# Layer 0 of a two-layer decoder trunk: tokens from a feature-major copy, first projection in a score bank, one insertion of attention work per projection

## The chip, the cores and the metric

The kernel runs on one core of one Trainium2 chip, in one launch. The metric is the device time of that core in microseconds (us). Engines: TensorE (PE; its weight loads, PEld, run beside its matmuls), VectorE (DVE), ScalarE (ACT), GpSimd (POOL), and the queue of SyncE (SP), which here only issues DMAs.

## The reference, cut to what matters

The input x is 256 tokens by 1024 features. Layer 0 is RMSNorm, stick-breaking attention with 16 heads of 64, a residual, then RMSNorm and a squared-ReLU MLP. Shared keys and values, a second layer of sparse attention with its own MLP, and a final norm follow; the change does not touch them.

```
def rms_norm(x, g):
    y = x * rsqrt(mean(x * x, axis=-1) + 1e-5)
    return y * g

def stick_breaking_attention(h, w_qkv, w_o):
    q, k, v = split(h @ w_qkv)                    # 16 heads of 64
    z = (q @ k.T) / 8                             # per head
    log_1m = where(causal, log_sigmoid(-z), 0)    # causal: key < query
    excl = reversed_cumsum(log_1m) - log_1m
    a = where(causal, exp(log_sigmoid(z) + excl), 0)
    return (a @ v) @ w_o

h = x + stick_breaking_attention(rms_norm(x, g0), w_qkv, w_o)
h = h + mlp(rms_norm(h, g1))
...
```

## The kernel before

Every large product is made of three: both factors are split into a high part that TensorE takes in one pass and the rest (h and l), and `mm3` (lines 131 to 134) adds h*h, h*l and l*h. Weights come from memory as f32 tiles `raw`; `split` (line 86) cuts one half of such a tile at a time: ScalarE casts it to `wh` (line 96), VectorE subtracts to `wl` (line 97). Each of the three has three buffers. `fetch` (line 75) issues the load of the next tile on SP; it is called when a tile's second half has been split, so the load waits until VectorE has read the tile three places ahead. `step` splits a half if the split is not yet three tiles ahead of the tile in use, `W(i)` splits up to tile i.

`layer0` (line 314) begins with eight matmuls on zeros (`warm`). Tokens are loaded token-major into `hres` in four pieces (line 337), which is also the residual. `xt_tr` (line 188) turns them on TensorE, 8 transposes per half of the features, and `xt_evac` (line 198) multiplies by the norm's gain out of PSUM and splits the result: ScalarE writes the high part (line 204), VectorE the rest (line 205), into `xa`. Then come two projections:

- Values: `v_proj(i)` (line 323) takes piece i of wv. `V_CUT` lists the pieces as (first slice, slices); a slice is 128 features. Per slice there are 12 matmuls of 512 columns, into four PSUM banks `pv`, one per 128 tokens t and half n of the output. Between, ScalarE squares `hres` with a sum (`sq`, line 176), VectorE makes the variance, GpSimd the power (`r`, line 185), and two small products (`pr`, line 361) spread 1/rms over the partitions, from which VectorE makes `rbq`. The four banks are then scaled into `v0` by ScalarE (line 367).
- Queries and keys: eight projections `proj(p)` (line 374), one per pair of heads, each 8 slices of 6 matmuls of 256 columns into one bank `qk`; VectorE scales it into `qkT` (line 385).

The attention of earlier pairs is put between the slices of a projection. `scores(p)` (line 388): TensorE makes z, VectorE caps it into `sbe` (line 404), ScalarE takes exp and ln(1+.) into `sbs` (lines 408, 409), VectorE scans it and subtracts (lines 410, 411), ScalarE takes the last exp (line 412). `turn(p)` (line 415): six transposes into two banks `pa`, copied to `sbt`, one by ScalarE and one by VectorE (lines 426, 424). `values(p)` (line 429): eight matmuls into `po`, split into `oT` by ScalarE and VectorE (lines 213, 214). `inside(n)` (line 441) says where: in projection n, before slice 2 the scores of pair n-1 and the values of pair n-3, before slice 5 the turn of pair n-2. What is left over stands in the output projection (line 454).

PSUM has 8 banks in two rings of four: `bank` (projections, pv, qk, acc) and `bank2` (z, pa, po, pt, pr and the MLP's pu). The order on an engine is made by a scheduler from the written order, and an engine runs its instructions strictly in that order.

## Time and profile before

| what | value |
|---|---|
| runs | 646.24 us median of 3 (646.06 to 646.59) |
| profiled execution | 646.55 us, of which the span from first to last instruction 644.8 us |
| TensorE (PE) busy | 625.1 us, 97% of the span |
| PE weight loads | 530.0 us, 82% |
| VectorE | 438.9 us, 68% |
| ScalarE | 347.5 us, 54% |
| GpSimd | 58.2 us, 9% |
| mean granted TensorE clock | 0.996 of full speed |
| DMA | 106.81 MB, 166 GB/s over the span |

Busy time is a union of instructions, so an engine that is 97% busy has 3% of gaps, and where they lie is read from stretches of the span, not from this table. A clock of 1.00 is 2.4 GHz and of 0.50 is 1.2 GHz. Starts in a timeline are us from the first instruction; a matmul's listed duration is longer than the distance to the next one's start, since matmuls overlap, so a cost per matmul is read from starts. A line's bracket tells how long the engine had stood idle and what ended that.

### The profile page before, as it was taken

Reading aid. Unit: us, or ns where it says so; the run is one execution under the profiler, and the core shown is the slowest. Engines: PE = TensorE matmul, PEld = TensorE weight load, DVE = VectorE, ACT = ScalarE, POOL = GpSimd, SP = SyncE. Lnnn points to the kernel's source line nnn. Section 1 sums busy time; section 2 is a strip of 40 time slices with the busy share of each in tenths; the row PEclk is TensorE's granted clock in tenths of the full one; section 3 lists DMA queues with packets and bytes.
Section 4 is the critical chain, followed back from the end, with each engine's and each line's share of the span. In section 5 each row is a group of like instructions: output and inputs, shape, how many; then the busy total and the mean of one; then the engine's idle time right before and its main releaser. Section 6 shows DMA issues by size and latency. Waiting matters only on the chain.

```text
span 644.8 us, 9082 instructions
## 1 busy us (share of the span) xinstructions
PE 625.1 (97%) x3552; PEld 530.0 (82%) x3552; DVE 438.9 (68%) x638; ACT 347.5 (54%) x596; POOL 58.2 (9%) x100
## 2 busy tenths in 40 slices
PE   8999899999999999999999999999999999999995
PEld 5889887888888888888889987777888888888884
DVE  4768887676666565656899879763776566656564
ACT  5665565564444544444847767762564444444433
POOL 1000000000000000000133344550000000000000
PEclk8999999999999999999999999999999999999999
DMA  8753223535555555553465752001545455555501
GB/s 304 282 226 132 104 100 125 195 131 201 200 187 199 193 196 195 194 195 134 142 241 177 254 191 82 18 2 66 190 148 206 176 201 188 196 197 195 197 0 66
DMA packets 16891, 106.81 MB, mean 166 GB/s; under 512 B 2256, under 2 KB 2512, under 8 KB 4944
## 3 DMA queue, kind: packets, MB, share of 16 engines
q1 hardware_dynamic: 15696, 104.92, 45.4%
q10 hardware_dynamic: 1152, 1.31, 0.6%
q8 instruction: 28, 0.46, 0.3%
q14 instruction: 15, 0.12, 0.1%
HBM read 105.17 MB, written 1.05 MB: 165 GB/s over the span
## 4 chain that ended last, share of the span: by engine, by line
PE 79%; DVE 10%; ACT 4%; issue 3%; POOL 2%; DMA 2%; POOLq 0%; SPq 0%; ACTq 0%; DVEq 0%
PE pu L137 27%; PE acc L132 11%; PE acc L133 11%; PE acc L134 11%; DVE wl L97 3%; PE po L137 2%; PE pk L134 2%; PE pk L132 2%; PE pk L133 2%; DVE sbs L410 2%; PE pv L132 1%; PE pv L133 1%; PE pv L134 1%; PE z L137 1%; ACT wh L96 1%
## 5 line engine op out<-in xcount | busy, mean ns | idle before, releaser
L97 DVE TENSOR_TENSOR wl<-raw,wh 128x1024 fp32r<-128x1024 f32 (+3 forms) x202 | 234.6, 1197 | 122.7 <-ACT wh L96 122.4
L96 ACT CAST wh<-raw 128x1024 fp32r<-128x1024 f32 (+3 forms) x202 | 198.1, 1024 | 119.5 <-PE acc L134 52.1
L137 PE MATMUL pu<-xn,wh 128*128 128x512 f32 x512 | 130.1, 392 | 0.6 <-DVE xn L205 0.6
L137 PEld LDWEIGHTS pu<-xn,wh 128*128 128x128 f32 x512 | 93.8, 188 | 19.6 <-DVE xn L205 1.8
L132 PE MATMUL acc<-wh,hh 128*128 128x512 f32 x256 | 100.2, 391 | 0.0
L133 PE MATMUL acc<-wl,hh 128*128 128x512 f32 x256 | 100.0, 391 | 0.0
L134 PE MATMUL acc<-wh,hl 128*128 128x512 f32 x256 | 99.5, 390 | 0.0
L137 PEld LDWEIGHTS pu<-xn,wl 128*128 128x128 f32 x512 | 71.0, 190 | 5.0
L137 PE MATMUL pu<-xn,wl 128*128 128x256 f32 x512 | 74.0, 282 | 0.0
L134 PEld LDWEIGHTS acc<-wh,hl 128*128 128x128 f32 x256 | 48.1, 188 | 10.6 <-DVE hl L294 0.4
L132 PEld LDWEIGHTS acc<-wh,hh 128*128 128x128 f32 x256 | 48.2, 188 | 9.6 <-ACT hh L293 0.6
L133 PEld LDWEIGHTS acc<-wl,hh 128*128 128x128 f32 x256 | 48.2, 188 | 8.8
L293 ACT CAST hh<-ms 128x512 fp32r<-128x512 f32 x32 | 19.9, 621 | 64.7 <-DVE ms L289 64.7
L287 ACT COPY mr<-pu 128x256 f32<-128x256 f32 x64 | 23.6, 369 | 28.9 <-PE pu L137 28.9
L132 PE MATMUL qk<-xa,wh 128*128 128x256 f32 x128 | 37.3, 291 | 0.0
L134 PE MATMUL qk<-xa,wl 128*128 128x256 f32 x128 | 36.3, 284 | 0.0
L133 PE MATMUL qk<-xa,wh 128*128 128x256 f32 x128 | 36.2, 283 | 0.0
L294 DVE TENSOR_TENSOR hl<-ms,hh 128x512 fp32r<-128x512 f32 x32 | 22.1, 692 | 19.9 <-ACT hh L293 19.9
L288 DVE TENSOR_TENSOR mu<-pu,mr 128x256 f32<-128x256 f32 x64 | 26.7, 418 | 5.8 <-ACT mr L287 5.8
L780 POOL TENSOR_TENSOR pe<-pe,rs 128x256 f32<-128x256 f32 (+1 forms) x32 | 27.1, 866 | 23.5 <-DVE rs L776 19.9
L132 PE MATMUL acc<-wh,oT 128*128 128x512 f32 x64 | 25.9, 405 | 0.0
L132 PEld LDWEIGHTS qk<-xa,wh 128*128 128x128 f32 x128 | 24.5, 191 | 1.0 <-issue 0.9
(188 smaller groups left out, 922.8 us busy)
## 6 DMA issues: line engine op xcount, KB each, us to landing
raw<-in_w SPq DMA_DIRECT2D x64, 1024.0 KB, 4.8
raw<-in_wqk SPq DMA_DIRECT2D x8, 1024.0 KB, 4.9
raw<-in_wo SPq DMA_DIRECT2D x8, 1024.0 KB, 4.8
raw<-in_wkv SPq DMA_DIRECT2D x6, 1024.0 KB, 4.8
raw<-in_cw SPq DMA_DIRECT2D x4, 1024.0 KB, 4.8
raw<-in_wv SPq DMA_DIRECT2D x3, 1024.0 KB, 6.4
raw<-in_wqb SPq DMA_DIRECT2D x2, 768.0 KB, 4.1
raw<-in_wqc SPq DMA_DIRECT2D x2, 768.0 KB, 6.1
```

Source lines behind the costliest of these rows:

```text
L96: nc.scalar.copy(h[:, r], raws[j][:, r])
L97: nc.vector.tensor_sub(lo[:, r], raws[j][:, r], f32(h[:, r]))
L132: nc.tensor.matmul(o, a[0], b[0], start=first, stop=False, skip_group_check=True)
L133: nc.tensor.matmul(o, a[0], b[1], start=False, stop=False, skip_group_check=True)
L134: nc.tensor.matmul(o, a[1], b[0], start=False, stop=last, skip_group_check=True)
L137: nc.tensor.matmul(o, a, b, start=first, stop=last, skip_group_check=True)
L287: nc.scalar.copy(r[:, q], pu[f][:, 256:512])
L288: nc.vector.tensor_add(u[:, q], pu[f][:, 0:256], r[:, q])
L293: nc.scalar.copy(hh, sv)
L294: nc.vector.tensor_sub(hl, sv, f32(hh))
L410: nc.vector.tensor_tensor_scan(s[:, ::-1], s[:, ::-1], go_on[:, ::-1], 0.0, OP.add, OP.mult)
L780: nc.gpsimd.tensor_tensor(s, s, rs[:, t, :][:, :, None].to_broadcast([P, 2, n]), op=OP.mult)
```

## The change

- The input gets a second layout, `xcols`: features on partitions, 8 slices of 256 tokens, made on the host from x. `x_load` brings slices 0 to 3 one by one (128 KB each) and 4 to 7 together into `xin`; `x_cut` multiplies by the gain and splits, from SBUF. The transposes of layer 0's first norm and their PSUM tiles go. There are 13 warm matmuls instead of 8.
- wv comes in six pieces instead of five (slices 0, 1, 2, 3 alone, then 4-5 and 6-7); from the third piece on two halves are split per slice; a slice runs output half by output half, with both token halves in each.
- `hres`, the constants and the identity are loaded on SP after the third piece's work is written; the identity came on ScalarE's queue before.
- The first projection's bank comes from `bank2`; the values' banks come from `bank`, but for the last two pairs.
- Scores, turn and values are put together, before slice 5 of a projection (slice 2 in projection 1); both copies of a turn are ScalarE's. The output projection takes the leftover of pairs 7, 6 and 5 in one place.

```diff
--- before.py
+++ after.py
@@ -24,7 +24,7 @@
 DFF = 4096
 NFC = 16
 NGN = 6
-V_CUT = ((0, 1), (1, 1), (2, 2), (4, 2), (6, 2))
+V_CUT = ((0, 1), (1, 1), (2, 1), (3, 1), (4, 2), (6, 2))
 EPS = 1e-5
 NEG = -1e30
 GELU_C = 2.0 * 0.7978845608028654
@@ -37,7 +37,7 @@
 
 
 @with_exitstack
-def hybrid_kernel(ctx, tc, x, eye, gcols, gfin, wqk, wv, wo0, wkv, wqa, wqb, wqc, wo1, w1, w2, cw1, cw2, cpos, gate_b, consts, out):
+def hybrid_kernel(ctx, tc, x, xcols, eye, gcols, gfin, wqk, wv, wo0, wkv, wqa, wqb, wqc, wo1, w1, w2, cw1, cw2, cpos, gate_b, consts, out):
     nc = tc.nc
 
     cp = ctx.enter_context(tc.tile_pool(name="cp", bufs=1))
@@ -156,7 +156,6 @@
     zero = cp.tile([P, 512], BF16, name="zero")
     nc.vector.memset(zero, 0.0)
     ident = cp.tile([P, P], F32, name="ident")
-    nc.scalar.dma_start(ident, eye)
     hres = [cp.tile([P, D], F32, name=f"hres{t}") for t in range(T)]
     gc = cp.tile([P, NGN * NK], F32, name="gc")
     nc.scalar.dma_start(gc, gcols)
@@ -314,7 +313,7 @@
     def layer0(ap):
 
         warm = bank2("warm")
-        for i in range(8):
+        for i in range(13):
             mm(warm, zero[:, 0:P], zero, True, True)
         xt = xt_tiles("a")
         v = big([P, T, D], F32, "v0")
@@ -324,27 +323,48 @@
             w = W(i_v[i])
             k0, m = V_CUT[i]
             for kk in range(m):
-                step()
+                step(2 if i >= 2 else 1)
                 k = k0 + kk
-                for t in range(T):
-                    for n in range(2):
+                for n in range(2):
+                    for t in range(T):
                         mm3(pv[t][n], tok(xt, k, t), cut(w, kk * D + n * 512, kk * D + (n + 1) * 512),
                             k == 0, k == NK - 1)
 
-        pts = []
-        for half in range(2):
-            for t in range(T):
-                nc.sync.dma_start(hres[t][:, half * 512:(half + 1) * 512], x[t * P:(t + 1) * P, half * 512:(half + 1) * 512])
-            fetch()
-        pts.append(xt_tr(0))
-        xt_evac(pts[0], 0, 0, xt)
+        xin = big([P, NK, T * P], F32, "xin")
+
+        def x_load(k, m):
+            nc.sync.dma_start(xin[:, k:k + m, :].rearrange("p k q -> p (k q)"), xcols[:, k * T * P:(k + m) * T * P])
+
+        def x_cut(k, m):
+
+            for k in range(k, k + m):
+                g = gc[:, k:k + 1]
+                nc.scalar.activation(xt[0][:, k, :], xin[:, k, :], AF.Copy, scale=g)
+                nc.vector.scalar_tensor_tensor(xt[1][:, k, :], xin[:, k, :], g, f32(xt[0][:, k, :]),
+                                               op0=OP.mult, op1=OP.subtract)
+
+        x_load(0, 1)
+        fetch()
+        x_load(1, 1)
+        fetch()
+        x_load(2, 1)
+        fetch()
+        x_load(3, 1)
+        x_cut(0, 1)
         W(i_v[0])
+        x_cut(1, 1)
+        v_proj(0)
+        x_load(4, 4)
+        x_cut(2, 1)
+        v_proj(1)
+        x_cut(3, 1)
+        v_proj(2)
         nc.sync.dma_start(cst, consts)
-        fetch()
-        pts.append(xt_tr(1))
-        v_proj(0)
-        v_proj(1)
-        xt_evac(pts[1], 1, 0, xt)
+        nc.sync.dma_start(ident, eye)
+        for t in range(T):
+            nc.sync.dma_start(hres[t], x[t * P:(t + 1) * P, :])
+        x_cut(4, 4)
+        v_proj(3)
         nc.gpsimd.tensor_copy(cbf, cst[:, 0:2 * P])
 
         go_on = ap.tile([P, 2 * ROW], BF16, name="go_on", bufs=1)
@@ -352,16 +372,15 @@
         nc.gpsimd.memset(go_on.rearrange("p (h c) -> p h c", h=2)[:, :, 2 * SEG - 1:ROW:SEG], 0.0)
         nc.gpsimd.tensor_copy(ident_r, ident)
         nc.gpsimd.tensor_copy(cmb, cst[:, C_CM:C_CM + 30])
-        v_proj(2)
+        v_proj(4)
         rstd = [rstd_of(hres[t]) for t in range(T)]
-        v_proj(3)
         rbq = ap.tile([P, 2, T * P], F32, name="rbq", bufs=1)
         pr = bank2("pr")
         for t in range(T):
             mm(pr[:, t * P:(t + 1) * P], rstd[t].to_broadcast([P, P]), ident, t == 0, True)
         nc.vector.tensor_scalar(rbq[:, 0, :], pr[:, 0:T * P], 0.125, None, op0=OP.mult)
         nc.vector.tensor_copy(rbq[:, 1, :], pr[:, 0:T * P])
-        v_proj(4)
+        v_proj(5)
         for t in range(T):
             for n in range(2):
                 nc.scalar.activation(v[:, t, n * 512:(n + 1) * 512], pv[t][n], AF.Copy, scale=rstd[t])
@@ -372,7 +391,8 @@
         live = {}
 
         def proj(p, hooks={}):
-            qk = bank("qk")
+
+            qk = bank("qk") if p else bank2("qk")
             w = W(i_qk[p])
             for k in range(NK):
                 if k % 4 == 0:
@@ -420,15 +440,12 @@
                 for i, b in enumerate((2, 0, 1)):
                     c = hd * ROW + b * SEG
                     nc.tensor.transpose(pt[:, i * P:(i + 1) * P], e[:, c:c + P], ident)
-                if hd:
-                    nc.vector.tensor_copy(at[:, hd, :], pt[:, 0:384])
-                else:
-                    nc.scalar.copy(at[:, hd, :], pt[:, 0:384])
+                nc.scalar.copy(at[:, hd, :], pt[:, 0:384])
             live[p] = at
 
         def values(p):
             a = live.pop(p)
-            po = bank2("po")
+            po = bank2("po") if p >= NP - 2 else bank("po")
             for b in range(2):
                 for hd in range(2):
                     r = slice(hd * DH, (hd + 1) * DH)
@@ -439,19 +456,12 @@
 
 
         def inside(n):
-            h = {}
-            if n >= 1:
-                h.setdefault(2, []).append(lambda: scores(n - 1))
-            if n >= 3:
-                h.setdefault(2, []).append(lambda: values(n - 3))
-            if n >= 2:
-                h.setdefault(5, []).append(lambda: turn(n - 2))
-            return h
+            return {2 if n == 1 else 5: [lambda f=f, p=n - d: f(p) for d, f in ((1, scores), (2, turn), (3, values)) if n >= d]}
 
         for n in range(NP):
             proj(n, inside(n))
         xn = xt_tiles("n")
-        out_proj(oT, i_o0, {(0, 0, 1): [lambda: scores(NP - 1), lambda: values(NP - 3)], (0, 0, 3): [lambda: turn(NP - 2)],
+        out_proj(oT, i_o0, {(0, 0, 2): [lambda: scores(NP - 1), lambda: turn(NP - 2), lambda: values(NP - 3)],
                             (0, 1, 1): [lambda: values(NP - 2)],
                             (1, 0, 0): [lambda: turn(NP - 1)], (1, 0, 1): [lambda: values(NP - 1)],
                             (1, 1, 2): [lambda: xt_evac(xt_tr(0), 0, 1, xn)]})
@@ -948,6 +958,7 @@
     wqs = [np.concatenate([wq[:, :256], wq[:, 1024:]], 1), wq[:, 256:640], wq[:, 640:1024]]
     f = {
         "x": cont(a["x"][0]),
+        "xcols": cont(a["x"][0].T.reshape(NK, P, T * P).transpose(1, 0, 2).reshape(P, NK * T * P)),
         "eye": np.eye(P, dtype=np.float32),
         "gcols": cont(np.concatenate([a["norm_gain"].reshape(4, D), a["kv_norm"][None], a["final_norm"][None]], 0)
                       .reshape(NGN, NK, P).transpose(2, 0, 1).reshape(P, NGN * NK)),
```

How this moves instructions shows at three places. First SP's queue at the start of the program, from the third issue on, before (x2 is two in a row):

```order
L81 DMA raw<-in_wv 128x512
L82 DMA raw<-in_wv 128x512
L337 DMA hres_72<-in_x 128x512
L337 DMA hres_73<-in_x 128x512
L84 DMA raw<-in_wv 128x1024
L84 DMA raw<-in_wv 128x2048
L342 DMA cst<-in_consts 128x744
L84 DMA raw<-in_wv 128x2048 x2
L84 DMA raw<-in_wqk 128x2048 x8
```

and now, from the eighth issue on:

```order
L336 DMA xin<-in_xcols 128x256
L84 DMA raw<-in_wv 128x1024
L336 DMA xin<-in_xcols 128x1024
L84 DMA raw<-in_wv 128x2048 x2
L84 DMA raw<-in_wqk 128x2048
L362 DMA cst<-in_consts 128x744
L363 DMA ident<-in_eye 128x128
L365 DMA hres_71<-in_x 128x1024
L365 DMA hres_72<-in_x 128x1024
L84 DMA raw<-in_wqk 128x2048 x7
```

The loads of the tokens for the residual (hres) stood at the head, two of the four ahead of these rows, and now stand behind all of wv, the first wqk, the constants (cst) and the identity; ahead of the rows stand now the first slice of xin, both halves of wv's first piece, and then slices of xin and pieces of wv in turn.

Second, VectorE in the middle of the projections, from one pair's cap (sbe from z) through its scan (sbs) to the next pair's cap, before:

```order
L404 TENSOR_TENSOR sbe_657<-z0_651,cst_76 128x3x128
L404 TENSOR_TENSOR sbe_657<-z1_652,cst_76 128x3x128
L214 TENSOR_TENSOR oT_320<-po_667,oT_320 128x256
L410 SCALAR_TENSOR_TENSOR sbs_661<-sbs_661,go_on_191 128x774
L424 COPY sbt_696<-pa_702 128x384
L411 TENSOR_TENSOR sbe_657<-sbe_657,sbs_661 128x774
L385 TENSOR_TENSOR qkT_725<-qk_634,rbq_278 128x512
L97 TENSOR_TENSOR wl_822<-raw_595,wh_821 128x1024
L404 TENSOR_TENSOR sbe_750<-z0_744,cst_76 128x3x128
L404 TENSOR_TENSOR sbe_750<-z1_745,cst_76 128x3x128
L97 TENSOR_TENSOR wl_822<-raw_595,wh_821 128x1024
```

and now:

```order
L424 TENSOR_TENSOR sbe_777<-z0_771,cst_75 128x3x128
L424 TENSOR_TENSOR sbe_777<-z1_772,cst_75 128x3x128
L213 TENSOR_TENSOR oT_325<-po_798,oT_325 128x256
L430 SCALAR_TENSOR_TENSOR sbs_781<-sbs_781,go_on_224 128x774
L405 TENSOR_TENSOR qkT_823<-qk_732,rbq_283 128x512
L431 TENSOR_TENSOR sbe_777<-sbe_777,sbs_781 128x774
L97 TENSOR_TENSOR wl_827<-raw_577,wh_826 128x1024 x2
L424 TENSOR_TENSOR sbe_870<-z0_864,cst_75 128x3x128
L424 TENSOR_TENSOR sbe_870<-z1_865,cst_75 128x3x128
```

The copy of the turn (sbt) is gone, qkT of the next pair stands ahead of the subtraction into sbe, and both halves of the weight (wl) stand ahead of the next cap; before, one of them stood behind the cap in this round, and both ahead of it in the next.

Third, ScalarE in the same place, from one pair's ln (the first row) to the next pair's ln (sbs is exp and ln, sbe the last exp), before:

```order
L409 ACTIVATE sbs_754<-sbs_754 128x774
L426 COPY sbt_789<-pa_790 128x384
L412 ACTIVATE sbe_750<-sbe_750 128x774
L96 CAST wh_914<-raw_688 128x1024 x2
L213 CAST oT_320<-po_853 128x256
L408 ACTIVATE sbs_847<-sbe_843 128x774
L409 ACTIVATE sbs_847<-sbs_847 128x774
```

and now:

```order
L429 ACTIVATE sbs_781<-sbs_781 128x774
L96 CAST wh_826<-raw_577 128x1024 x2
L432 ACTIVATE sbe_777<-sbe_777 128x774
L443 COPY sbt_880<-pa_881 128x384
L443 COPY sbt_880<-pa_886 128x384
L428 ACTIVATE sbs_874<-sbe_870 128x774
L212 CAST oT_325<-po_891 128x256
L429 ACTIVATE sbs_874<-sbs_874 128x774
```

The weight's casts (wh) stand between ln and the last exp, two turn copies follow that, and the cast of oT stands between exp and ln. Before, there was one turn copy, behind ln, the casts stood behind the last exp, and the cast of oT ahead of exp.

## Rows read from the trace of the kernel before

**Rows 1.** Windows: busy us (instructions) of PE, PEld, DVE, ACT, POOL; clock, DMA, GB/s.
```profile
60.00:80.00 20.00, 18.10 (x154) 16.73 (x153) 16.48 (x21) 11.17 (x16) 0.32 (x3) 1.00 0.36 124
```

**Rows 2.** Timeline of the start: start us, duration, engine, line, instruction, [idle before].
```profile
0.73 0.86 SPq L337 DMA_DIRECT2D hres<-in_x  x2
...
1.19 3.52 PE L137 MATMUL warm<-zero 128*128 128x512 bf16 x8 [1.19 <-DVE zero L157]
...
5.15 0.98 PE L195 MATMUL pt<-ident,hres 128*128 128x128 f32 x7 [0.33 <-DMA hres<-in_x]
...
6.67 0.62 ACT L96 CAST wh<-raw 128x512 fp32r<-128x512 f32 x1 [4.66 <-DMA raw<-in_wv]
...
7.71 0.64 PE L132 MATMUL pv<-wh,xa 128*128 128x512 f32 x1 [1.58 <-ACT xa L204]
...
12.42 0.39 PE L132 MATMUL pv<-wh,xa 128*128 128x512 f32 x1
...
17.84 1.06 ACT L176 ACTIVATE sq<-hres 128x1024 f32<-128x1024 f32 x1
...
19.69 1.16 POOL L185 TENSOR_TENSOR r<-v,cst 128x1 f32<-128x1 f32 x2 [5.27 <-DVE v L180]
```

**Rows 3.** Windows of one microsecond at the start, columns as in rows 1.
```profile
6.00:7.00 1.00, 0.13 (x2) 0.00 (x0) 0.00 (x0) 0.33 (x1) 0.00 (x0) 1.00 1.01 289
...
8.00:9.00 1.00, 1.00 (x5) 0.75 (x4) 1.00 (x4) 1.00 (x4) 0.00 (x0) 0.50 0.99 336
...
11.00:12.00 1.00, 1.00 (x7) 0.91 (x7) 0.25 (x1) 0.75 (x2) 0.00 (x0) 0.83 0.91 374
```

**Rows 4.** Timeline of PE through the projections, columns as in rows 2.
```profile
32.62 0.28 PE L132 MATMUL qk<-xa,wh 128*128 128x256 f32 x1
...
38.37 0.28 PE L132 MATMUL qk<-xa,wh 128*128 128x256 f32 x1
...
59.62 0.82 PE L422 MATMUL pa<-ident,sbe 128*128 128x128 f32 x6
...
60.19 0.36 PE L132 MATMUL qk<-xa,wh 128*128 128x256 f32 x1
...
64.16 0.92 PE L137 MATMUL z<-qkT 64*128 64x256 f32 x8
...
65.01 0.87 PE L137 MATMUL po<-sbt,v 128*64 128x256 f32 x8
...
65.81 0.39 PE L132 MATMUL qk<-xa,wh 128*128 128x256 f32 x1
...
74.25 0.92 PE L137 MATMUL z<-qkT 64*128 64x256 f32 x8 [1.77 <-DVE qkT L385]
...
98.71 0.40 PE L132 MATMUL acc<-wh,oT 128*128 128x512 f32 x1
```

**Rows 5.** Timeline of DVE through the projections, columns as in rows 2.
```profile
65.35 2.36 DVE L97 TENSOR_TENSOR wl<-raw,wh 128x1024 fp32r<-128x1024 f32 x2 [1.25 <-ACT wh L96]
...
67.62 1.02 DVE L404 TENSOR_TENSOR sbe<-z,cst 128x384 f32<-128x384 f32 x2
...
70.50 1.77 DVE L410 TENSOR_TENSOR_SCAN sbs<-sbs,go_on 128x774 f32<-128x774 f32 x1 [1.53 <-ACT sbs L409]
...
72.19 0.53 DVE L424 COPY sbt<-pa 128x384 f32<-128x384 f32 x1
...
72.64 0.96 DVE L411 TENSOR_TENSOR sbe<-sbe,sbs 128x774 f32<-128x774 f32 x1
...
73.51 0.68 DVE L385 TENSOR_TENSOR qkT<-qk,rbq 128x512 f32<-128x512 f32 x1
...
103.08 1.02 DVE L404 TENSOR_TENSOR sbe<-z,cst 128x384 f32<-128x384 f32 x2
```

**Rows 6.** Timeline of ACT through the projections, columns as in rows 2.
```profile
66.17 0.36 ACT L213 CAST oT<-po 128x256 fp32r<-128x256 f32 x1
...
68.74 0.85 ACT L408 ACTIVATE sbs<-sbe 128x774 f32<-128x774 f32 x1 [2.21 <-DVE sbe L404]
```

## The prediction

> **What bounds the kernel now.** I read the windows first, then the timeline of the start, then the timelines of the three busy engines through layer 0's projections. From 60 to 80 us TensorE is busy 18.10 of 20 us, VectorE 16.48 and ScalarE 11.17 [rows 1]: TensorE has gaps there, and VectorE, which shows 82%, is the one to suspect. The rest of the kernel is matmul back to back, so what the change saves before the first MLP should stay saved; I found no later wait that would swallow some us.
>
> The start: the first matmul that counts, pv, begins at 7.71, after a 1.58 us wait for ScalarE's token cut, and at 12.42 the tenth starts [rows 2]. From there to the first qk at 32.62 [rows 4] 87 pv and the small pr group take 20.20 us, 0.232 us per pv. The nine before took 4.71 us instead of 9 x 0.232 = 2.09: 2.6 us lost, to transposes in between, waits for the first cuts, and the clock.
>
> The projections: from 32.62 to 98.71 [rows 4] eight of them take 66.1 us. TensorE's own work in them: a projection is 48 matmuls in 5.75 (32.62 to 38.37), a z group costs 0.85 (64.16 to 65.01), a po group 0.80 (to 65.81), a pa group 0.57 (59.62 to 60.19) [rows 4]. With 7 z, 5 po and 6 pa: 46.0 + 5.95 + 4.0 + 3.4 = 59.4. So 6.7 us are waits; the longest shown is z waiting 1.77 for qkT [rows 4]. Behind it is VectorE's order. Its round from one cap of scores to the next takes (103.08 - 67.62) / 4 = 8.87 us [rows 5], where a full TensorE period is 5.75 + 0.85 + 0.80 + 0.57 = 7.97. In the round VectorE stands idle 1.25 us for weight casts and 1.53 us for exp and ln [rows 5].
>
> **The change, part by part.**
>
> *Tokens from xcols.* The 16 transposes ahead of pv go, and ScalarE and VectorE cut from SBUF, eight pairs as before. The first half weight is now second on SP's queue, behind 128 KB. Before, it was third, behind 512 KB; it let ScalarE start at 6.67, and pv followed 1.04 later [rows 2]. The nearest row for the new place is the second 256 KB load of before, also issued second (0.73, two issues in 0.86), which let TensorE go on at 5.15 [rows 2]. So the first pv comes at 5.15 + 1.04 = 6.2. Bounds: 7.7 (nothing gained) and 5.5 (if half the bytes ahead matter). Then 96 pv and pr: 96 x 0.232 = 22.3. Of the 2.6 us lost, the transposes go, the clock should stay up (below), and the waits for VectorE's first cuts stay: I take a third, 0.8, between ends of 0 and 2.6. First qk at 6.2 + 22.3 + 0.8 = 29.3, against 32.62: **3.3 us** earlier. By the ends: 5.5 + 22.3 = 27.8 to 7.7 + 22.3 + 2.6 = 32.6.
>
> The Trainium skill has a rule for such a load ("DMA: Bandwidth & Descriptors", the section on the two cost components): about 2 us plus the bytes at 436 GB/s, given for the other descriptor path. An estimate from it lands that half weight 2.6 us after its issue at 1.16, at 3.8, and would make the start 1.4 us better still. The trace disagrees: the load of that size in that place released TensorE only at 5.15, so the sum keeps the row.
>
> *Five more warm matmuls.* The eight take 3.52 us, 0.44 each, about half the rate of the later pv; the granted clock was 1.00 from 6 to 7, but 0.50 (1.2 GHz) from 8 to 9, and 0.83 from 11 to 12 as it came back [rows 3]. Before it fell, TensorE had been busy 0.13 of a microsecond from 6 to 7 [rows 3]. Five more reach to 6.9 at 0.44, or 5.8 at twice the rate, so pv follows almost directly and I expect no fall. They cost nothing: TensorE has no data then.
>
> *Residual tokens, consts and ident late.* hres is now issued behind all of wv and the first wqk. Who needs it: sq, then r on GpSimd, then pr, which stands on TensorE behind all pv. From sq's start at 17.84 to r's end at 20.85 it took 3.0 us [rows 2]. Bytes up to hres: 1.05 MB xcols, 4.19 wv, 1.05 wqk, 0.45 consts and ident, 1.05 hres, together 7.8 MB. At 289 GB/s [rows 3] from 2 us on, that ends at 29; at 374 [rows 3], at 22.9. I take 25 (the fuller rate holds once loads are large), so r is ready at 28, before the last pv at about 29: no cost. Above 26, each us is a us of TensorE idle, and ScalarE, queued behind sq, casts the second wqk later; that has 5.75 us of slack, one projection. The sixth piece of wv costs one more issue, and the sizes of the pieces hide in the same stream.
>
> *One insertion per projection.* z, pa and po now stand together at slice 5. Two things follow. qkT gains three slices, 3 x 0.72 = 2.2 us, so z's waits (1.77 for one) go. In their place pa of a pair comes one full period after its z: 7.97 us later. What must fit between: cap, exp and ln, 2.88 (67.62 to 70.50 [rows 5]), with the oT cast, 0.33 of it exposed (0.36 long [rows 6]), now between them; the scan 1.69, qkT 0.61 (now ahead of the subtract), the subtract 0.87 [rows 5], and the last exp 0.85, as long as the first [rows 6], with 0.1 for the hand-overs: 7.33. That leaves 0.64 of slack.
>
> *The turn's copy to ScalarE, casts ahead of the last exp.* VectorE loses a copy, 0.45 (72.19 to 72.64), and the 1.25 idle for casts [rows 5], since ScalarE casts while VectorE scans. Its round becomes 2.88 + 0.33 + 1.69 + 0.61 + 0.87 + 2.27 (two wl, 65.35 to 67.62 [rows 5]) = 8.65. That is more than 7.97: VectorE still sets the pace, and TensorE waits 0.68 per period, now at pa for the last exp. The slack delays it once: between the second and third z there is no po yet (7.17), VectorE needs 8.32, the lag of 1.15 exceeds 0.64 by 0.5; then four periods at 0.68. Waits 0.5 + 2.7 = 3.2 instead of 6.7: 3.5 us gained. The output projection pays part back, since z and pa of the last pairs meet the lag again: I take one to two waits of 0.68, 1.0. Net **2.5 us**, ends 0 (round as before) and 6.7 (TensorE's own pace).
>
> *Banks.* qk of the first projection in a score bank and po in projection banks: the score banks then turn over 4 a period for 4 buffers. No wait on a bank shows in the rows, so I put it at nothing; what covers it is that caps and copies end long before the next insertion. Without that cover, pa would wait for a cap, 0.5 per period.
>
> Sum: 3.3 + 2.5 = 5.8. The profiled execution took 646.55 with a span of 644.8; less 5.8 it is 640.75, and the median of the runs stands 0.31 below it: **640.4**.
>
> **The rivals.**
> 1. *The clock falls at the start anyway.* Pv starts in bits, and the granted clock fell in before, too, after partial work. In the Trainium skill, "TensorE: Matmul & The Clock Gate" (table "Why this matters for your kernels") ties a drop to a long idle gap; by that rule the forecast stands. Here it fell after a gap of 1.58 us, so the row speaks for this rival. Price: half rate from 8 to 11.4, 1.7 us less half a us that waits there would have cost anyway, 1.2: 641.6.
> 2. *The loop gains nothing.* ScalarE now has two turn copies and the oT cast ahead of ln; if they delay exp by 0.2 per round, the round is 8.87 again and only the start is gained: 642.9. For it: VectorE's round hardly falls. Against: the copies wait on pa, which ends before the caps do.
> 3. *TensorE reaches its own pace in the loop*: another 3.2 gone, 637.2. Against it: 8.65 over 7.97.
> 4. *Slower: the residual tokens come too late.* Place: pr, behind the last pv, and all of ScalarE behind sq. It decides from a landing after 29, where the start's gain is used up (r at 32). At 31: r at 34, first qk at 34.5, 1.9 worse; TensorE idle for 5 us starts again at half clock, 1.7; the value evacuation and the third pair's casts then delay the first z by about 1.1; less the loop's 2.5: +2.2, 648.4. For it: a megabyte more ahead, in an interval where the queues are always full. Against: 289 GB/s held only in the first microseconds.
>
> **How the numbers follow.** A difference of 0.2%, 1.3 us, is about what a measurement of this kernel can tell from none. Chances: forecast 0.54 (639.2 to 641.4), rival 1 0.19, rival 2 0.13, rival 3 0.07, rival 4 0.07. Faster by over 0.2% means below 644.9: forecast, 1 and 3, most of 2, together 0.88; within 0.2% 0.06 (the weak end of 2, the mild end of 4); slower 0.06. For 8 in 10 the range reaches from 638.4, the forecast's better end with a little of rival 3, to 644.4, rival 2 with a start 1.5 worse.
>
> **What would show it.** Right: first pv near 6.2, first qk near 29.3, no wait before pr, granted clock 1.00 from 8 to 11; no z wait for qkT in the middle projections, pa waiting about 0.7 for the last exp in each, caps 8.65 apart, the output projection starting some 62.6 after the first qk. Wrong: a TensorE wait at pr for r of over 1 us, caps 8.9 or 8.0 apart, or waits of pa or po for a bank.

## The result, and the profile after

The changed kernel took 641.07 us (median of four runs: 642.27, 639.96, 640.21, 641.93) against 646.25 (646.06 to 646.59) of the kernel before: a ratio of 0.992, with a 95% interval of 0.9897 to 0.9942. That is 5.2 us less; the forecast was 640.4. The profiled execution is the slowest of the four, 642.27, with a span of 640.4, so it stands 4.28 below that of before, 4.4 by the spans. One of the seven executions of the last experiment, the profiled one, had a mean granted clock of 0.85 and took 688.36 us, and one of the kernel before beside the experiments took 3523.38; both are left out, and nothing is read from the trace of the first.

Three instants cut the path of TensorE:

| us | before | after, profiled | after, a second profiled execution |
|---|---|---|---|
| first qk | 32.62 | 31.20 | 28.95 |
| output projection starts (first acc) | 98.71 | 93.58 | 91.53 |
| MLP starts (first pu) | 126.83 | 122.65 | 120.59 |
| the eight projections, qk to acc | 66.09 | 62.38 | 62.58 |
| the output projection, acc to pu | 28.12 | 29.07 | 29.06 |

The second execution is that of an experiment below, beside which the kernel before had a median of 645.46. So the start gave 1.42 in one execution and 3.67 in the other, the projections 3.7 and 3.5, and the output projection took 0.95 back. From the first pu to the end of the span it is 518.0 before and 517.8 after: what was saved stayed saved.

The windows of after, in the stretch of [rows 1] and in the first microseconds of [rows 3], with two more (busy us of PE, PEld, DVE, ACT, POOL, then clock, DMA share, GB/s):

```profile
60.00:80.00 20.00, 20.00 (x169) 18.44 (x168) 16.55 (x19) 13.07 (x19) 0.22 (x2) 1.00 0.37 138
...
6.00:7.00 1.00, 1.00 (x4) 0.64 (x3) 1.00 (x3) 0.58 (x2) 0.00 (x0) 1.00 0.96 327
8.00:9.00 1.00, 1.00 (x6) 0.81 (x6) 0.11 (x1) 0.76 (x2) 0.00 (x0) 1.00 1.06 397
11.00:12.00 1.00, 1.00 (x6) 0.84 (x5) 1.00 (x3) 0.43 (x1) 0.00 (x0) 1.00 1.06 352
...
15.00:16.00 1.00, 1.00 (x7) 0.80 (x6) 1.00 (x4) 0.67 (x2) 0.00 (x0) 1.00 0.65 147
```

TensorE has no gap left from 60 to 80 (18.10 busy before), the clock stays at 1.00, and in one microsecond the DMAs move 147 GB/s, less than half of what the other rows of the start show. The timeline of after's start and output projection, PE, ACT and POOL (columns as in [rows 2]):

```profile
1.19 5.73 PE L137 MATMUL warm<-zero 128*128 128x512 bf16 x13 [1.19 <-DVE zero L157]
6.36 0.94 PE L132 MATMUL pv<-wh,xa 128*128 128x512 f32 x1
...
19.46 1.19 PE L132 MATMUL pv<-wh,xa 128*128 128x512 f32 x4 [1.50 <-ACT wh L96]
...
30.83 0.61 PE L137 MATMUL pr<-ident,r 128*128 128x128 f32 x4
31.20 0.36 PE L132 MATMUL qk<-xa,wh 128*128 128x256 f32 x1
...
93.58 0.40 PE L132 MATMUL acc<-wh,oT 128*128 128x512 f32 x1
...
98.15 0.88 PE L442 MATMUL pa<-ident,sbe 128*128 128x128 f32 x6 [0.80 <-ACT sbe L432]
...
122.65 0.39 PE L137 MATMUL pu<-xn,wh 128*128 128x512 f32 x1
...
5.16 0.50 ACT L342 ACTIVATE xa<-xin,gc 128x256 fp32r<-128x256 f32 x1
...
18.37 2.00 ACT L96 CAST wh<-raw 128x1024 fp32r<-128x1024 f32 x2 [2.70 <-DMA raw<-in_wv]
...
25.68 1.06 ACT L175 ACTIVATE sq<-hres 128x1024 f32<-128x1024 f32 x1 [0.34 <-DMA hres<-in_x]
...
28.38 0.55 POOL L184 TENSOR_TENSOR r<-v,cst 128x1 f32<-128x1 f32 x1 [0.73 <-DVE v L179]
```

The first pv shows no wait: it stands behind the last of the 13 warm matmuls, although ScalarE's first cut, xa, had ended at 5.66. The values stop for 1.50 us at the fifth piece of wv, whose cast waited for its load; pr follows the last pv directly, since r was ready at 28.93. One round of the loop in after, first PE, then VectorE, then ScalarE:

```profile
63.68 0.92 PE L137 MATMUL z<-qkT 64*128 64x256 f32 x8
64.53 0.88 PE L442 MATMUL pa<-ident,sbe 128*128 128x128 f32 x6
65.34 0.87 PE L137 MATMUL po<-sbt,v 128*64 128x256 f32 x8
66.14 0.39 PE L132 MATMUL qk<-xa,wh 128*128 128x256 f32 x1
...
72.08 0.92 PE L137 MATMUL z<-qkT 64*128 64x256 f32 x8
...
65.73 1.02 DVE L424 TENSOR_TENSOR sbe<-z,cst 128x384 f32<-128x384 f32 x2
67.99 0.42 DVE L213 TENSOR_TENSOR oT<-po,oT 128x256 fp32r<-128x256 f32 x1 [1.24 <-ACT oT L212]
68.74 1.77 DVE L430 TENSOR_TENSOR_SCAN sbs<-sbs,go_on 128x774 f32<-128x774 f32 x1 [0.33 <-ACT sbs L429]
70.43 0.67 DVE L405 TENSOR_TENSOR qkT<-qk,rbq 128x512 f32<-128x512 f32 x1
71.01 0.96 DVE L431 TENSOR_TENSOR sbe<-sbe,sbs 128x774 f32<-128x774 f32 x1
71.88 2.35 DVE L97 TENSOR_TENSOR wl<-raw,wh 128x1024 fp32r<-128x1024 f32 x2
74.15 1.02 DVE L424 TENSOR_TENSOR sbe<-z,cst 128x384 f32<-128x384 f32 x2
...
63.58 0.85 ACT L432 ACTIVATE sbe<-sbe 128x774 f32<-128x774 f32 x1 [1.41 <-DVE sbe L431]
...
66.84 0.85 ACT L428 ACTIVATE sbs<-sbe 128x774 f32<-128x774 f32 x1 [0.87 <-DVE sbe L424]
```

TensorE's round is 72.08 - 63.68 = 8.40 with no idle time in it, VectorE's 74.15 - 65.73 = 8.42, where it was 8.87 by [rows 5]; that is the mean of rounds of 7.6 and 10.1 us in turn. VectorE follows one chain, cap, (exp and ln on ScalarE), scan, qkT, subtract, two wl, cap, and waits only for ScalarE, 1.57 us. The last exp ends at 64.43 and pa starts at 64.53, so the two engines meet there.

TensorE's waits between first qk and first acc (us in total, times, longest), before:

```profile
PE z L137 <- DVE qkT L385: 4.4, 4, 1.8
```

and after:

```profile
PE pa L442 <- ACT sbe L432: 0.3, 1, 0.3
```

So TensorE's own work in the eight projections was 66.1 - 4.4 = 61.7 before and is 62.4 - 0.3 = 62.1 after.

### The profile page after: what moved, and what is told of

Same layout as the page of the kernel before. It is cut to its first block, busy times and chain, and to the rows that moved or that the text cites. A ratio compares the mean times of both kernels' runs of the same rounds, so it can differ in the third digit from the quotient of the medians.

```text
span 640.4 us, 9068 instructions
## 1 busy us (share of the span) xinstructions
PE 624.8 (98%) x3541; PEld 527.9 (82%) x3541; DVE 435.6 (68%) x632; ACT 350.5 (55%) x606; POOL 59.6 (9%) x100
## 3 DMA queue, kind: packets, MB, share of 16 engines
q10 hardware_dynamic: 1008, 1.25, 0.5%
## 4 chain that ended last, share of the span: by engine, by line
PE 75%; DVE 12%; ACT 4%; DMA 4%; issue 3%; POOL 1%; SPq 0%; POOLq 0%; ACTq 0%; DVEq 0%
PE pu L137 27%; PE acc L132 11%; PE acc L133 11%; PE acc L134 11%; DVE wl L97 5%; PE po L137 2%; DMA raw<-in_wv 2%; DVE sbs L430 2%; PE pk L134 2%; PE pk L132 2%; PE pk L133 2%; ACT wh L96 1%; DVE sbe L424 1%; ACT sbs L429 1%; ACT sbs L428 1%
```

## The experiments

The experiments ran on four chips. The kernel before had medians of 645.28 to 645.53 beside them, and one more execution of the changed kernel took 639.91.

### The start alone and the loop alone

The first keeps the loop, its copies, places and banks as before, and takes the start of the change; the second takes the loop and keeps the start of before. In both the first projection stands in a score bank.

> The start of the change alone (tokens from xcols, six pieces of wv, 13 warm products, hres late, first qk in a score bank); scores, turn and values where they were before. Theory A (start and loop add up): first qk near 31.2 us as in the changed kernel, or near 29.2 where the fifth piece of wv comes in time, output projection 66.1 after it as before, so 1.4 to 3.4 us below the kernel before. Rival B (the loop's gain comes only from the start's slack): output projection about 62.5 after the first qk, over 4 us below before.

> The loop of the change alone (one insertion at slice 5, both turn copies on ScalarE, po in projection banks), with the start as before. Theory A: first qk at 32.6 as before, caps 8.4 apart, output projection 62.4 after the first qk, its own stretch 0.9 longer than before: 2.8 us below before. Rival B: caps 8.8 to 8.9 apart and within 1 us of before.

The start alone took 643.81 (ratio 0.998, 0.9967 to 0.9992), the loop alone 641.36 (0.9947, 0.9927 to 0.9966). With the start alone the first qk came at 29.10, 3.5 earlier than in the profile of before, but the loop took 67.1, 1.0 more than before, with 5.3 us of waits for qkT where before had 4.4. From first qk to first acc, PE's waits, start alone:

```profile
PE z L137 <- DVE qkT L405: 5.3, 5, 1.8
```

With the loop alone the eight projections took 62.08 and the output projection 29.06: the loop's gain of 3.7 to 4.0 and the 0.95 given back are the loop's own. So Theory A holds: the two parts add up, and the loop needs nothing of the new start. Which of the start's own changes (tokens from xcols, the cut of wv, the late residual) gives its gain, no run separates. The kernel with the loop alone has the start of before, eight warm matmuls and transposes included, and its clock did not fall. Windows and the first qk, loop alone:

```profile
6.00:7.00 1.00, 0.19 (x2) 0.00 (x0) 0.01 (x1) 0.66 (x2) 0.00 (x0) 1.00 1.00 348
8.00:9.00 1.00, 1.00 (x7) 0.76 (x7) 1.00 (x4) 0.99 (x3) 0.00 (x0) 1.00 1.07 422
...
30.86 0.28 PE L132 MATMUL qk<-xa,wh 128*128 128x256 f32 x1
```

Its first qk is 1.76 earlier than that of before, where the clock was 0.50 in the second of these windows [rows 3]; 0.32 of that is there at the first pv already (7.39). So the start of before has two outcomes, and against the better one the new start is worth 1.9 (30.86 to 28.95), not 3.7. The times without a trace fit this, though a mean clock does not tell where the clock fell: with the loop alone, three executions at a mean clock of 0.998 took 640.89 to 641.50 and one at 0.994 took 643.39; of the executions of the kernel before beside the experiments, 14 at 0.997 or more have a median of 644.60, 41 at 0.996 or less one of 645.67.

### The fifth piece of the values' weight

The third kernel cuts that piece in two, the fourth is the changed kernel once more.

```diff
-V_CUT = ((0, 1), (1, 1), (2, 1), (3, 1), (4, 2), (6, 2))
+V_CUT = ((0, 1), (1, 1), (2, 1), (3, 1), (4, 1), (5, 1), (6, 2))
```

> The changed kernel with the fifth piece of wv (slices 4 and 5) cut into two pieces of one slice. Theory A (TensorE waits 2 us at slice 4 because a 1 MB load issued at 10.6 lands at 18.3, shared with the load behind it): half of it lands near 16.5, the wait at slice 4 falls below 0.5, first qk near 29.4, and the spread of the runs shrinks; 640 us or a little less. Rival C (the wait is ScalarE's order, token cuts ahead of the cast): the wait stays at 1.5 to 2, first qk at 31.2, same time as the changed kernel.

> The changed kernel again, one look, because its four runs lie in two pairs 2 us apart. Theory A: the pairs differ by the wait at slice 4 alone, so a run near 640 shows the first qk near 29.2 with no wait there, and a run near 642 shows it at 31.2. Rival D: they differ elsewhere (clock, or a late load in the MLPs), with the first qk at the same place in both.

Cut in two: 641.03 (640.14 to 642.45), no wait at slice 4, first qk at 29.18, though two short waits appear earlier, 0.47 and 0.22. That the cut did this is not shown, since the wait is also absent from the nine other traces of the new start in which the piece is whole. The changed kernel again, ACT's cast of the fifth piece and the first qk:

```profile
15.36 2.00 ACT L96 CAST wh<-raw 128x1024 fp32r<-128x1024 f32 x2 [0.85 <-DMA raw<-in_wv]
...
28.95 0.36 PE L132 MATMUL qk<-xa,wh 128*128 128x256 f32 x1
```

The cast that began at 18.37 began here at 15.36, TensorE did not wait there, and the first qk stands 2.25 and the first pu 2.06 earlier. The DMAs issued from 10 to 20 us (KB each, median us to landing), in the late execution:

```profile
raw<-in_wv SPq DMA_DIRECT2D x2, 1024.0 KB, 8.1
```

and in this one:

```profile
raw<-in_wv SPq DMA_DIRECT2D x2, 1024.0 KB, 5.5
```

The first of the two was issued at 10.61 in both. The same load of the same kernel lets its cast begin 3.0 us later in one execution, and that is the 2 us between these two: the last pv before that piece starts at 17.57 in the one and 17.48 in the other. The piece ahead of it was late too, its cast at 12.74 against 11.61. Why the DMAs moved 147 GB/s in that microsecond, no run shows; and as the finer cut also has a run at 642.45, which has no trace, it is no cure for the spread.

### The clock at the start

```diff
-        for i in range(13):
+        for i in range(8):
```

> The changed kernel with 8 warm-up matmuls instead of 13; everything else of the change stays. Theory A (the clock term of the prediction): without the last five, which cost nothing because the first value matmul waits for its data until 5.5 to 6.4 us, TensorE stands still from about 4.7 us to the first pv, and the granted clock can fall to 0.50 afterwards as it did in the kernel before (from 8 to 11.4 us); then each matmul of 512 columns takes 0.43 instead of 0.21 in that stretch, the first scores matmul comes 1.7 us later than in a like run of the change (about 30.7 with the fifth value piece in time, 32.9 with it late) and the time is about 1.7 above: 641.6 to 643.7. Rival B: eight are enough, the clock stays at 1.00 from 6 us on; then the time is that of the change, 640 to 642, and the first scores matmul at 28.9 to 31.2.

640.15 (639.47 to 640.72). TensorE stood still for a microsecond before the first pv, and the clock was at 1.00 from 4 to 20 us:

```profile
5.50 0.72 PE L132 MATMUL pv<-wh,xa 128*128 128x512 f32 x2 [1.00 <-ACT xa L342]
...
8.00:9.00 1.00, 1.00 (x5) 0.41 (x3) 0.67 (x1) 0.80 (x3) 0.00 (x0) 1.00 1.00 327
```

First qk 28.23. Rival B holds: with eight the clock stayed up, and the five more bought nothing that these executions show. One of the four, 640.72, has a mean clock of 0.994 and no trace; the others have 0.997 to 0.999. Nor are the five shown to be free: with 13 the first pv of the changed kernel started at 6.36 and 5.47, right behind the last of them both times, and here at 5.50 as soon as its data came. At the first qk, 28.23 stands just below the 28.50 to 29.49 of the eight traces with 13 and no wait at the fifth piece or for a bank.

### The banks

First the first projection back in a value bank, then the values' accumulator back in the score banks.

```diff
-            qk = bank("qk") if p else bank2("qk")
+            qk = bank("qk")
...
-            po = bank2("po") if p >= NP - 2 else bank("po")
+            po = bank2("po")
```

> The changed kernel with the first projection's accumulator back in one of the four value banks; the rest stays. Theory A: the four value banks are held until their copies to the values, which need the second r (28.4 to 28.9 us) and come after the last pv; the first scores matmul waits for the first of these copies, about 1.5 to 3 us behind pr, and the first scores matmul comes at 31 to 33 us in a run with the fifth value piece in time; the time is 1.5 to 3 us above the change. Rival B (the prediction put the bank at nothing): the wait falls beside something that is late anyway, such as the weight pieces of the first projections, and the time is within 0.5 us of the change, 640 to 642.

> The changed kernel with the values' accumulator po back in the score banks for every pair; the rest stays. The prediction put the choice of bank at nothing, with 0.5 us per period if pa had to wait for a cap. Theory A: z, pa and po need 5 score banks a round for 4 buffers, so that po or the next z waits for a copy of the same round: waits of 0.3 to 0.8 us on TensorE in six rounds, and the time is 2 to 4 us above the change. Rival B (banks at nothing): no wait on a bank shows, and the time is 640 to 642.

The first: 642.29 (ratio 0.996, 0.9941 to 0.9979), and the wait that theory A names:

```profile
32.84 0.57 PE L132 MATMUL qk<-xa,wh 128*128 128x256 f32 x1 [2.92 <-ACT v L386]
```

Behind that wait the granted clock fell to 0.50, from 33 to 36 us, and the loop took 63.68, 1.1 to 1.3 more than with the change. This execution, 645.14, is one of the two slowest of ten; the other eight took 641.31 to 643.31.

The second: 642.0 (0.9942, 0.9925 to 0.996), the loop 64.31 instead of 62.4 to 62.6; a new wait stands once, while the loop fills, not in six rounds:

```profile
56.06 0.87 PE L137 MATMUL po<-sbt,v 128*64 128x256 f32 x8 [0.98 <-DVE sbe L424]
```

From the first z, at 36.65, the loop took 56.16, where after took 55.01, so the bank's part is 1.15. The rest is a wait of 0.72 of that first z for qkT, ahead of the first po; the traces with eight warm matmuls and with one copy on VectorE show such a wait too, 0.32 and 0.94.

In the traces each choice of bank saves a wait, 2.9 and 1.0 us; in the medians it is 1 to 2 us each, about as much as the runs of one kernel spread. Theory A is right on the first bank, and on the second only in that there is a wait.

### What sets the round

Five kernels. One of the turn's copies back on VectorE:

```diff
-                nc.scalar.copy(at[:, hd, :], pt[:, 0:384])
+                if hd:
+                    nc.vector.tensor_copy(at[:, hd, :], pt[:, 0:384])
+                else:
+                    nc.scalar.copy(at[:, hd, :], pt[:, 0:384])
```

> The changed kernel with one of the turn's two copies back on VectorE (0.45 a round), as the kernel before had one. Theory A (the prediction's term: VectorE's own work sets the round): the round between cap copies goes from 8.42 to about 8.87 us, eight rounds cost 3.2 to 3.6 us, and the time is 643.5 to 645. Rival B: the copy falls into the time in which VectorE waits anyway (1.24 us for the copy of oT and 0.33 for the scan), the round stays at 8.4 to 8.5 and the time at 640 to 642.5: then the moved copy bought nothing, and the gain of the loop comes from the places of the insertions and of the values' accumulators alone.

641.81 (0.9944, 0.9922 to 0.9966). VectorE, from one cap to the next:

```profile
73.14 1.01 DVE L424 TENSOR_TENSOR sbe<-z,cst 128x384 f32<-128x384 f32 x2
74.07 0.54 DVE L444 COPY sbt<-pa 128x384 f32<-128x384 f32 x1
75.39 0.42 DVE L213 TENSOR_TENSOR oT<-po,oT 128x256 fp32r<-128x256 f32 x1 [0.77 <-ACT oT L212]
...
81.55 1.02 DVE L424 TENSOR_TENSOR sbe<-z,cst 128x384 f32<-128x384 f32 x2
```

8.41, the same: the copy falls into the wait for ScalarE, 0.77 instead of 1.24. Rival B holds. The loop as a whole took 63.39, with one 0.94 us wait for qkT at its beginning, at 37.56; but that is ahead of the first turn, and from this first z to the first acc it took 55.01, as in after (38.57 to 93.58). So the moved copy bought nothing.

The old places (scores and values ahead of slice 2, the turn ahead of slice 5, and the old places in the output projection), all else as changed:

> The changed kernel with the insertions back in two places of each projection (scores and values ahead of slice 2, the turn ahead of slice 5), while the copies stay on ScalarE, the values in projection banks and the start as changed. Theory A (the places make the gain of the loop): the score matmul waits again for the copy of the projection, 1.8 to 2.5 us in most of seven rounds, the round is 8.7 or more and the time 642.5 to 645. Rival B (the copy on ScalarE and the banks make the gain): VectorE's round stays at 8.4, TensorE waits in another place for the same total, and the time is 640 to 642.

645.5 (1.0002, 0.9992 to 1.0012): the whole gain is gone, although the first qk came at 28.96. The loop took 66.95 and the output projection 29.72, 0.65 more than with the change. PE's rows, and its waits in the loop:

```profile
70.62 0.92 PE L137 MATMUL z<-qkT 64*128 64x256 f32 x8 [1.39 <-DVE qkT L405]
...
74.52 0.82 PE L442 MATMUL pa<-ident,sbe 128*128 128x128 f32 x6
75.10 0.36 PE L132 MATMUL qk<-xa,wh 128*128 128x256 f32 x1
...
PE z L137 <- DVE qkT L405: 5.2, 6, 1.5
```

The waits for qkT are back, and so are VectorE's 1.25 us for the casts of the weight. Theory A: the places make the loop's gain. The copies and the banks of the values are what this kernel has ahead of the one with the start alone, and the loop is 67.1 there and 66.95 here, so with the old places they are worth 0.2. In this kernel pa, ahead of a qk, costs 0.58.

VectorE without its wl of projections 3 to 7 (the third product then counts the high part of these weights a second time):

```diff
+        if i_qk[3] <= j <= i_qk[-1]:
+            made[j] = (h, h)
+        else:
+            nc.vector.tensor_sub(lo[:, r], raws[j][:, r], f32(h[:, r]))
```

> The changed kernel without VectorE's low parts of the weights (wl) of projections 3 to 7, five times two halves of 1.14 us; the third matmul of each of these products reads the high part in their place, so that these weights are computed with less precision and TensorE does the same number of matmuls. Theory A (what sets the round of 8.42 now is the chain cap, exp, oT copy, ln, scan, qkT, subtract, two wl, each behind the one before): with 2.27 less in it TensorE sets the round from the third projection on, at its own pace of 7.97 (48 matmuls 5.75, z 0.85, pa 0.57, po 0.80) to 8.2, and pa no longer starts 0.07 us behind the end of the last exp; four to five rounds give 0.8 to 2.2 us. Rival B: TensorE is at its own pace already (it shows hardly an idle nanosecond in a round); the round stays at 8.4 and the loop at 62.6 us after the first scores matmul.

VectorE's caps, two in a row, now wait for z:

```profile
63.20 1.02 DVE L427 TENSOR_TENSOR sbe<-z,cst 128x384 f32<-128x384 f32 x2 [2.03 <-PE z L140]
...
71.59 1.02 DVE L427 TENSOR_TENSOR sbe<-z,cst 128x384 f32<-128x384 f32 x2 [2.03 <-PE z L140]
```

VectorE has 2 us to spare and the round is 8.39. Rival B: TensorE is at its own pace, and that pace is 8.40, not 7.97. The loop took 62.65, from its first z 54.67 where after took 55.01. In the output projection, which took 28.19 instead of 29.07, pa no longer waits: what that projection gave back comes from VectorE. The two executions took 639.60 and 640.16.

One wl half per projection on GpSimd, from projection 3 to the second weight piece of the output projection (not the fourth):

```diff
-        nc.vector.tensor_sub(lo[:, r], raws[j][:, r], f32(h[:, r]))
+        eng = nc.gpsimd if half == 0 and i_qk[3] <= j <= i_o0[0][1] else nc.vector
+        eng.tensor_sub(lo[:, r], raws[j][:, r], f32(h[:, r]))
```

> The changed kernel with one of the two halves of the low weights of projections 3 to 7 and of the first four pieces after them on GpSimd instead of VectorE; nothing is left out. GpSimd does nothing else in the loop but a 0.11 us fill. Theory A (VectorE's chain sets the round): VectorE loses 1.14 a round, GpSimd needs some 3.5 us for a half and has 8; the round falls from 8.42 towards TensorE's own pace, 8.0 to 8.2, and the time by 1 to 2 us against the change. Rival B: the half on GpSimd comes late for the projection that needs it, or slows VectorE beside it; TensorE waits for wl, 0.5 us or more in several rounds, and the time is the same or worse. Rival C: TensorE is at its own pace already, the time stays at 640 to 642.

647.59 (1.0035, 1.0023 to 1.0046), slower than both kernels. GpSimd, then VectorE:

```profile
73.85 2.41 POOL L98 TENSOR_TENSOR wl<-raw,wh 128x1024 fp32r<-128x1024 f32 x1 [4.01 <-ACT wh L96]
...
74.49 2.58 DVE L432 TENSOR_TENSOR sbe<-sbe,sbs 128x774 f32<-128x774 f32 x1
```

VectorE's subtract, 0.96 in after, takes 2.58 and ends at 77.07, 0.81 after GpSimd's half ends at 76.26: for most of that time it stood. In the next two rounds it takes 2.84, and the caps come 9.28 apart. TensorE's waits in the loop:

```profile
PE pa L443 <- ACT sbe L433: 4.8, 4, 2.4
PE z L138 <- DVE qkT L406: 2.4, 2, 1.9
```

Rival B holds in its second half, a VectorE slowed by GpSimd; TensorE did not wait for wl. Behind the longest of these waits, which ended at 58.86, the granted clock fell to 0.50 from 61 to 63 us, so part of the 71.3 us of this loop is the clock.

The last: the turn two slices behind the rest, at slice 7.

```diff
-            return {2 if n == 1 else 5: [lambda f=f, p=n - d: f(p) for d, f in ((1, scores), (2, turn), (3, values)) if n >= d]}
+            h = {}
+            if n >= 1:
+                h.setdefault(2 if n == 1 else 5, []).append(lambda: scores(n - 1))
+            if n >= 3:
+                h.setdefault(5, []).append(lambda: values(n - 3))
+            if n >= 2:
+                h.setdefault(7, []).append(lambda: turn(n - 2))
+            return h
```

> The changed kernel with the turn (pa) two slices behind the scores and the values of the same projection, at slice 7, from the third projection on; its other parts stay. Theory A (the round is set twice, by TensorE's own 8.40 us and by VectorE's chain of 8.42, as the runs before this one say): a pa that stands ahead of a projection's matmuls costs 0.57 in place of 0.80 ahead of po, so TensorE's own round becomes 8.2; and ScalarE copies oT ahead of the first exp instead of between exp and ln, which takes 0.25 out of VectorE's chain, 8.17. Both fall, the caps come 8.2 apart, the loop takes 61.2 to 61.8 us from the first scores matmul instead of 62.4 to 62.6, and the time is 0.6 to 1.2 below the change, 639 to 641. Rival B: only one of the two falls; the caps stay 8.4 apart and the time within 0.4 of the change. Rival C: two places cost TensorE or ScalarE more than they save (the casts of the weights now stand behind the two copies of the turn): a new wait for wl or for sbt, and the time is 1 us or more above the change.

Six executions of 639.11 to 641.22, median 639.90, ratio 0.9918 (0.9903 to 0.9933). Rival C is out. Between A and B it stays open: the interval overlaps that of the change, and no trace shows the round.

## Why the prediction was right, point by point

- **The sum**: 5.8 forecast, 5.2 measured between the medians. By parts the forecast had 3.3 for the start and 2.5 for the loop; the two executions gave 1.4 and 3.7 for the start, 2.8 and 2.6 for the loop with what the output projection took back. Against the better outcome of the start of before, the new start gave 1.9 at best. That the sum came out near is in part luck, in both halves.
- **First pv** 6.2 forecast, 6.36 measured (5.47 in the second execution). The forecast took it from when the data come, and they were there at 5.66; what held pv until 6.36 were the 13 warm matmuls, of which the prediction says that they cost nothing. So this agreement is chance. **First qk** 29.3 forecast, 31.20 and 28.95. The step that failed in the slower execution is "the sizes of the pieces hide in the same stream": one large piece landed late and TensorE paid about 2 us. What the first cuts cost behind the first pv, 0.8 forecast, was 1.2 in the second execution (23.48 from pv to qk, less 22.3).
- **The clock** held in both traces (rival 1 wrong for these), but the argument for the five more matmuls is not borne out: with eight it held too, after a 1.00 us wait, and so it did with the start of before after 1.20 us, where the profile of before shows a fall after 1.58 us [rows 2, 3]. So the start of before can go either way; the two executions differ in that wait, and no run shows what decides. Length alone does not: the clock held behind 1.77 in the loop of before [rows 4] and behind 1.86, at 48.02, in the trace with GpSimd, and fell behind the waits of 2.36 there and 2.92 with the value bank. The table of the Trainium skill ("TensorE: Matmul & The Clock Gate", "Why this matters for your kernels"), which ties a drop to a long idle gap, agrees with after and with both experiments on the start and not with the fall in before.
- **hres** 25 forecast, 25.68 measured; r 28, measured 28.93; no wait at pr. Rival 4 was far off.
- **The places**: z's waits went, as forecast, and the experiment with the old places shows that this is where the loop's gain is.
- **The loop's sum** was right by luck, with two wrong terms that cancel. The own work of TensorE, put at 59.4, was too small: it is 61.7 before. So the waits to be won were 4.4, not 6.7, and 0.3 is left of them, not 3.2: 4.1 won, not 3.5, less the 0.4 by which TensorE's own work grew. The step that says VectorE still sets the pace, with pa waiting 0.68 per period, did not hold; pa waited once, 0.25. A period of TensorE was put at 7.97 and is 8.40: pa was priced at 0.57 from a row where a qk follows it [rows 4], and between z and po it takes 0.81 (between z and qk, at 48.39 in after, 0.63); and the 48 matmuls between two insertions take 5.94 (66.14 to 72.08) where the first projection, without one, takes 5.75. Rival 3 named the right state, TensorE at its own pace, with the wrong pace.
- **VectorE's round** 8.65 forecast, 8.42 measured: cap to scan took 3.01, not 2.88 + 0.33. It and TensorE's 8.40 are so near each other that relieving VectorE alone gave 0.3 in the loop and 0.9 behind it. "VectorE loses a copy, 0.45" counted for nothing in the round, as that copy stood beside a wait.
- **The payback** of the output projection, 1.0 forecast, 0.95 measured, 0.80 of it the one pa wait at 98.15.
- **The banks**, "at nothing": right as a cost of the change, but they are not idle choices. With the new order the old banks cost waits of 2.9 and 1.0 us in the traces.

## What to carry to other kernels

Price an instruction group from a row with the same neighbours, and check the sum of an engine's own work against its span less the waits shown: here 59.4 against 61.7 would have told at once that 2.3 us of "waits" were work. Before relieving an engine, ask whether its own instructions or its waits fill the round; a copy taken from an engine that then waits is worth nothing, while changing what stands ahead of what was worth over 4 us. Where a kernel's times lie 2 us apart, look in both profiles for one load that comes late, and at the granted clock of the first microseconds.

## What the hardware showed that I had not expected

- GpSimd and VectorE did not work side by side on such operands: a subtract of two SBUF tiles, 0.96 us alone, took 2.58 while GpSimd subtracted for 2.41, and finished 0.81 after it. The Trainium skill says so ("SBUF — State Buffer", "Who interferes with whom"): a VectorE instruction with two SBUF inputs contends with a GpSimd one that reads SBUF, and it calls the contention for the ports that they share an exclusive lock. The trace agrees.
- The same six transposes cost TensorE 0.58 between two qk, 0.63 between z and qk and 0.81 between z and po: most of the difference goes with what follows them.
- A load of 1 MB issued at the same instant, 10.61 us, let its cast begin 3.0 us later in one execution than in another; in one microsecond there the DMAs moved 147 GB/s.
- The granted clock fell to 0.50 for some 3 us behind single waits of TensorE of 1.58, 2.36 and 2.92 us, and did not behind others of up to 1.86.
